# Gate products of a gated MLP as filler beside attention, with their gelu built from tanh

## The chip, the cores and the metric

The kernel runs on one core of a Trainium2 chip. The metric is the device time of one launch in microseconds, as the median of three runs. TensorE (PE) multiplies, VectorE (DVE), ScalarE (ACT) and GpSimd (POOL) work on its results, and SyncE (SP) issues the DMAs. Each engine works through its own queue of instructions in order and waits on semaphores where an instruction needs another engine's result.

## The reference

Two transformer blocks of two layers each, width 1024, float32. The first block mixes three attention branches and a convolutional feed-forward. The second, where most of the change lies, has 256 latent and 256 context tokens; in its last layer the context gives keys and values alone. The gated branch `chunk_gmlp` and the attention share one output product:

```python
def chunk_gmlp(u, vg, w_s, b_s, g_norm):
    u = gelu(u)
    vg = group_layernorm(gelu(vg).reshape(b, n, 4, 128), g_norm)     # 4 groups of 128
    mixed = einsum('gpq,bnqgc->bnpgc', w_s, chunks of 128 rows of vg) + b_s
    return u * mixed.reshape(b, n, 512)

for l in range(2):
    z = modulate(rmsnorm(x), ...) @ w_in[l]          # q | k | v | u | vg
    attn = softmax(q k^T) v                          # 8 query heads of 64, 2 kv heads, after rmsnorm and rope
    x = x + gate1 * (concat([attn, chunk_gmlp(u, vg, ...)]) @ w_out[l])
    x = x + gate2 * (relu(modulate(rmsnorm(x), ...) @ w_ff1[l])**2 @ w_ff2[l])
```

## The kernel before

**Products.** Every float32 product is three TensorE products of operands split into a rounded part hi and a remainder lo (`mm3`: L157 hi by hi, L158 and L159 with one lo). Weights come as raw tiles of 128x2048 into three buffers (`load_w`); ScalarE casts pieces of 1024 columns to hi (L147) and VectorE subtracts to get lo (L149). Activations are split the same way by `split` (L181 on ScalarE, L182 on VectorE). Products of a layer's weights go to PSUM tiles called acc, scores to s, transposed probabilities to pt, attention output to o.

**Order.** The program is written as Python generators, and a scheduler puts each engine's instructions in order, the earlier traced with the higher priority, as operands come free. `weave(main, side, ratio)` draws steps of a filler `side` after each step of `main`, `ratio` of them on average, and what is left at the end.

**A layer of block 2.** After q, k and v come the products of vg, in two halves of two groups (`g_half`, 4 row tiles of 128 in layer 0, 2 in layer 1; a Gelu on ScalarE for each, L970). Then VectorE takes mean and variance of every group (bn_stats L1049, bn_aggr L1050), a reciprocal root is formed on POOL, and the groups are normalised (L1055). `u_tasks` makes the four gate tiles of u: for each, 8 contraction steps of 3 products for each stream (latents, and in layer 0 context too), so 192 products of 256 columns in layer 0 and 96 in layer 1, and one Gelu on ScalarE (L1066). All four are traced ahead of attention. Then `weave(attn(), fill, WV2[l])` runs attention, 16 steps in layer 0 and 8 in layer 1, with a filler: four mix tiles (`mix_tasks`, 32 or 16 small products L1077, then the gate's factor L1083 and a split) and the half of w_out's products that reads the gated branch (`out_half(1)`, eight tiles). The other half, `out_half(0)`, follows attention.

**An attention step.** For a pair of heads and a block of queries: scores s (six products), their maximum (L1099 or L1103, VectorE), its scaling (L1107), exp on ScalarE with its sum (L363), the sum's reciprocal (L371), the scaling of the probabilities on ScalarE (L374), and `pair_out`: four transposes into pt (L388), a split of pt (L181, L182) and six products with v into o, as many rounds as there are pairs of key blocks. `pair_out` serves block 1 too.

Other lines: L257 are modulation products on VectorE, which are traced as side work (`prep`, `mod_rate`), L1044 the final norm's factors of block 1's output.

Of the kernel before, what the change touches and what calls it, by code (L numbers as in the profile page):

```python
# [19 lines left out]
P = 128  # L20
# [16 lines left out]

PIN = (False, True, True, False)

WV2 = (0.78, 1.62)  # L40

NMR = 2

# [4 lines left out]
WL = (1.0, 0.75)  # L48

PIPE = 1  # L50

WV = (0.34, 1.48, 0.48)

# [18 lines left out]
def program(tc, A, out, stop=None):  # L72
# [4 lines left out]
    def mk(pool, shape, dtype=F32, tag=None, bufs=None):  # L77
        count[0] += 1
        kw = {} if bufs is None else {"bufs": bufs}
        return pool.tile(shape, dtype, tag=tag, name=f"{tag}_{count[0]}", **kw)  # L80

    top = ExitStack()
    with top:
# [205 lines left out]
        def cut(s):  # L289
            return slice(s * T, (s + 1) * T)  # L290
# [27 lines left out]
        def run(gen):  # L318
            for _ in gen:
                pass  # L320
# [58 lines left out]
        def pair_out(po, ps, v, n):  # L379

            for g in range(0, n, 2):
                pt = mk(pst, [P, 512], tag="pt")
                for k in range(2):
                    for i in range(2):
                        o = (2 * k + i) * P
                        PE.transpose(pt[:, o : o + P], ps[i][:, (g + k) * P : (g + k + 1) * P], ident)  # L388
                hi, lo = mk(top_pt[0], [P, 512], F32R, **top_pt[1]), mk(top_pt[0], [P, 512], F32R, **top_pt[2])
                split(pt, hi, lo)  # L390
                for k in range(2):
                    c = slice(k * T, k * T + T)
                    mm3(po, v(g + k), (hi[:, c], lo[:, c]), g + k == 0, g + k == n - 1)

        def pair_split(po, hi, lo):

# [429 lines left out]
        def block2():  # L826
            with ExitStack() as st:
# [32 lines left out]
                def mm_x(ps, piece, x, n):  # L860
                    mm_w(ps[:, 0:n], piece, 0, KD, lambda k: x(k, slice(0, n)))
# [9 lines left out]
                for l in range(L):  # L871
# [89 lines left out]
                    def g_half(c, w):  # L961
                        if not vg:
                            vg.append(u8([P, 4, 512]))
                        for b in range(NB):
                            ps = acc()[:, :T]
                            x, bs = (hl, hc)[b // 2], slice(b % 2 * P, b % 2 * P + P)
                            for k in range(KD):
                                mm3(ps, x(k, bs),
                                    at(w[k // 4], slice(None), slice(k % 4 * T, k % 4 * T + T)), k == 0, k == KD - 1)
                            S.activation(vg[0][:, b, c * T : (c + 1) * T], ps, AF.Gelu_apprx_tanh)  # L970
                            yield

                    if l == 0:
                        hc, e, al, wk = glob["start"]
# [62 lines left out]
                    for _ in g_half(0, wg):  # L1037
                        next(prep, None)
                    wu = load_w(A["w_in2"][l, 3], 1024, 2048)
                    weave(g_half(1, wg2), prep, 1.0)  # L1040
                    vg = vg[0]
                    if l == 0:
                        for k in range(KD):
                            V.scalar_tensor_tensor(xx[:, k, LAT], xx[:, k, LAT], glob["fing"][:, k : k + 1], frow[:, 0, :], op0=ALU.mult, op1=ALU.mult)  # L1044
                    mv = mk(kp, [P, 4, 4, 2], tag="mv", bufs=1)
                    for b in range(NB):
                        for g in range(4):
                            bn = small([P, 6], tag="bn", bufs=2)
                            V.bn_stats(bn, vg[:, b, g * P : (g + 1) * P])  # L1049
                            V.bn_aggr(mv[:, b, g, :], bn)  # L1050
                    rv = rsqrt(mv[:, 0:NB, :, 1], [P, NB, 4], 1.0, EPS)
                    for b in range(NB):
                        for g in range(4):
                            gs = slice(g * P, (g + 1) * P)
                            V.tensor_scalar(vg[:, b, gs], vg[:, b, gs], mv[:, b, g, 0:1], rv[:, b, g : g + 1],  # L1055
                                            op0=ALU.subtract, op1=ALU.mult)
                    u = u8([P, 4, 512])

                    def u_tasks():
                        for c in range(2):  # L1060
                            w = load_w(A["w_in2"][l, 4], 1024, 2048) if c else wu
                            for mi in range(2):
                                ps = acc()
                                for s in streams:
                                    mm_x(ps[:, cut(s)], w[mi], (hl, hc)[s], T)
                                S.activation(u[:, 2 * c + mi, full], ps[:, full], AF.Gelu_apprx_tanh)  # L1066
                                yield


                    gm = []  # L1070

                    def mix_tasks():
                        gm[:] = [u8p()]
                        for g in range(4):
                            ps = acc()[:, :N]
                            for b in range(NB):
                                PE.matmul(ps[:, b * P : (b + 1) * P], vg[:, b, g * P : (g + 1) * P], wsT[:, g, :], start=True, stop=True)  # L1077
# [5 lines left out]
                            V.tensor_mul(t[:, :N], t[:, :N], u[:, g, full])  # L1083
                            split(t[:, :N], *gm[0](g, full))
                            yield


                    def attn():
# [59 lines left out]
                    def gate(m, ps, cols):  # L1148
                        update(m, ps, 2, cols)

                    fill = chain(mix_tasks(), out_half(1, lambda k, c: gm[0](k, c), gate))
                    run(u_tasks())
                    mod_rate(R2[1])
                    ya = u8p()
                    weave(attn(), fill, WV2[l])

                    def products(ap, x, cols_list, use, first=None):
# [215 lines left out]
```

## Time and profile before

| | |
|---|---|
| median of 3 runs | 1806.24 us (1802.46, 1806.24, 1807.23) |
| the profiled execution | 1804.39 us, span 1802.6 us |
| mean granted TensorE clock | 0.993 |
| PE, DVE, ACT busy | 97%, 80%, 56% of the span |
| layer 0's attention in block 2 | 1000.0 to 1098.6 us |
| layer 1's attention in block 2 | 1533.4 to 1607.3 us |

The two stretches run from the first scores to the first products with finished attention output. PE busy is the union of the matmuls' modelled durations; matmuls overlap, so their number in a window says more than their busy time. DVE and ACT busy times are sums over instructions that don't overlap.

### The profile page before, as it was taken

The numbers are of one execution on the slowest core, as the hardware profiler recorded it, in microseconds if no ns is written. First come the engines' busy times: TensorE is split into PE (matmuls) and PEld (weight loads), VectorE is DVE, ScalarE is ACT, GpSimd is POOL, SyncE is SP. The second block draws the span as 40 slices with busy tenths as digits, with TensorE's granted clock in tenths as the row PEclk, the third lists the DMA queues.
The fourth block names the chain that finished last, engine by engine and source line by source line (L and its number), as shares of the span: only waits on it lengthen the run. The fifth ranks groups of instructions, "written<-read, shape, count | busy, mean of one in ns | idle before, by whom it ended". The sixth has DMA issues, their size and how long they took to land.

```text
span 1802.6 us, 33988 instructions
## 1 busy us (share of the span) xinstructions
PE 1750.1 (97%) x13352; PEld 1669.1 (93%) x13352; DVE 1449.8 (80%) x3142; ACT 1014.0 (56%) x1994; POOL 83.0 (5%) x85
## 2 busy tenths in 40 slices
PE   7999999999999999999999899999999999799999
PEld 6999999999999999999999677989898989689999
DVE  7996989889898788988778676988676768777665
ACT  5866656665585665766554575515151536665553
POOL 0100210000010021000012000000000001000000
PEclk9999999999999999999999999999999999999999
DMA  7364664557545456554533221554545443225552
GB/s 283 123 212 165 211 233 171 186 164 257 197 159 199 163 183 246 185 190 158 195 138 119 71 71 36 168 201 154 185 149 191 141 151 117 71 72 209 187 187 94
DMA packets 68096, 297.10 MB, mean 165 GB/s; under 512 B 7648, under 2 KB 11104, under 8 KB 42336
## 3 DMA queue, kind: packets, MB, share of 16 engines
q1 hardware_dynamic: 67936, 294.93, 47.4%
q8 instruction: 105, 1.72, 0.4%
q14 instruction: 55, 0.45, 0.1%
HBM read 293.85 MB, written 1.05 MB: 164 GB/s over the span
## 4 chain that ended last, share of the span: by engine, by line
PE 82%; DVE 9%; ACT 5%; issue 2%; POOL 1%; DMA 1%; SPq 0%; POOLq 0%; ACTq 0%; DVEq 0%
PE acc L157 24%; PE acc L158 23%; PE acc L159 23%; DVE lo L149 2%; PE s L157 2%; PE s L158 2%; PE s L159 2%; PE pt L388 1%; ACT hi L147 1%; DVE u L182 1%; PE o L158 1%; ACT p L363 1%; DVE mjunk L257 1%; ACT p L374 1%; PE o L157 1%
## 5 line engine op out<-in xcount | busy, mean ns | idle before, releaser
L157 PE MATMUL acc<-u,hi 128*128 128x256 f32 (+2 forms) x3604 | 1052.3, 293 | 17.5 <-ACT hi L147 10.3
L159 PE MATMUL acc<-u,lo 128*128 128x256 f32 (+2 forms) x3604 | 1048.7, 292 | 2.6 <-DVE lo L149 2.4
L158 PE MATMUL acc<-u,hi 128*128 128x256 f32 (+2 forms) x3604 | 1051.0, 292 | 0.0
L147 ACT CAST hi<-raw 128x1024 fp32r<-128x1024 f32 (+2 forms) x470 | 473.6, 1010 | 452.9 <-PE acc L158 383.8
L157 PEld LDWEIGHTS acc<-u,hi 128*128 128x128 f32 x3604 | 682.6, 190 | 33.5 <-ACT hi L147 11.4
L159 PEld LDWEIGHTS acc<-u,lo 128*128 128x128 f32 x3604 | 682.4, 190 | 16.7 <-DVE lo L149 4.2
L158 PEld LDWEIGHTS acc<-u,hi 128*128 128x128 f32 x3604 | 683.6, 190 | 13.6 <-DVE u L182 0.6
L149 DVE TENSOR_TENSOR lo<-raw,hi 128x1024 fp32r<-128x1024 f32 (+2 forms) x470 | 552.0, 1182 | 104.5 <-ACT hi L147 100.7
L257 DVE CUSTOM_DVE_ANT_0 mjunk<-mraw,csil,c_par 128x512 bf16<-128x512 f32 x160 | 120.7, 754 | 10.5 <-DMA mraw<-in_w_mod 9.8
L257 DVE CUSTOM_DVE_ANT_0 mjunk<-mraw,csil,mpart 128x512 bf16<-128x512 f32 x160 | 120.8, 755 | 7.9 <-DMA mraw<-in_w_mod 6.5
L1130 DVE SCALAR_TENSOR_TENSOR xx<-acc,mods,xx 128x256 f32<-128x256 f32 x144 | 64.7, 479 | 55.4 <-PE acc L159 55.2
L868 ACT ACTIVATE nt<-nt,shb 128x256 f32<-128x256 f32 x96 | 48.7, 510 | 61.0 <-DVE nt L867 60.9
L181 ACT CAST u<-nt 128x256 fp32r<-128x256 f32 x146 | 57.3, 405 | 41.0 <-DVE nt L1212 33.3
L195 POOL TENSOR_TENSOR rs_y<-rs_v,mhalf 128x2 f32<-128x2 f32 (+2 forms) x26 | 30.9, 1188 | 1019.3 <-DVE rs_v L193 1019.3
L182 DVE TENSOR_TENSOR u<-nt,u 128x256 fp32r<-128x256 f32 x146 | 59.4, 421 | 17.0 <-ACT u L181 15.6
L159 PE MATMUL s<-u,lo 128*128 128x256 f32 x224 | 62.9, 281 | 0.5 <-DVE lo L149 0.5
L157 PE MATMUL s<-u,hi 128*128 128x256 f32 x224 | 62.7, 280 | 0.0
L158 PE MATMUL s<-u,hi 128*128 128x256 f32 x224 | 62.7, 280 | 0.0
L1212 DVE TENSOR_TENSOR nt<-nt 128x256 f32<-128x256 f32 x96 | 40.5, 423 | 19.1 <-ACT nt L868 13.1
L157 PE MATMUL acc<-hi,u 128*128 128x256 f32 (+1 forms) x168 | 48.6, 289 | 0.0
L182 DVE TENSOR_TENSOR kf<-pt,kf 128x512 fp32r<-128x512 f32 x40 | 27.5, 688 | 26.2 <-ACT kf L181 26.0
L159 PE MATMUL acc<-hi,u 128*128 128x256 f32 (+1 forms) x168 | 48.2, 287 | 0.0
(243 smaller groups left out, 2048.7 us busy)
## 6 DMA issues: line engine op xcount, KB each, us to landing
raw<-in_w_ff SPq DMA_DIRECT2D x64, 1024.0 KB, 4.9
raw<-in_w_in SPq DMA_DIRECT2D x61, 1024.0 KB, 4.9
mraw<-in_w_mod SPq DMA_DIRECT2D x192, 256.0 KB, 3.4
raw<-in_w_up SPq DMA_DIRECT2D x44, 1024.0 KB, 4.9
raw<-in_w_down SPq DMA_DIRECT2D x32, 704.0 KB, 4.2
raw<-in_w_out SPq DMA_DIRECT2D x16, 1024.0 KB, 4.9
raw<-in_w_br SPq DMA_DIRECT2D x12, 1024.0 KB, 4.9
nbias<-in_na_bias SPq DMA_DIRECT2D x8, 384.0 KB, 3.0
```

The costliest lines, as they stand in the source:

```text
L147: S.copy(hi[:, : b - a], raw[:, a:b])
L149: last_lo[0] = V.tensor_sub(lo[:, : b - a], raw[:, a:b], hi[:, : b - a].bitcast(F32))
L157: PE.matmul(ps, a[0], b[0], start=start, stop=False)
L158: PE.matmul(ps, a[0], b[1], start=False, stop=False)
L159: return PE.matmul(ps, a[1], b[0], start=False, stop=stop)
L181: S.copy(hi, src)
L182: return V.tensor_sub(lo, src, hi.bitcast(F32))
L195: G.tensor_tensor(y, v, mhalf[:, :n] if len(shape)==2 else mhalf[:, :n].rearrange('p (a b) -> p a b', b=shape[2]), op=ALU.pow)
L257: V.tensor_tensor_reduce(out=junk, in0=w, in1=csil[:, i, half * 512 : half * 512 + 512], op0=ALU.mult, op1=ALU.add, scale=1.0, scalar=part ...
L868: S.activation(dst, dst, func, bias=b)
L1130: V.scalar_tensor_tensor(xx[:, m, cut(s)], ps[:, s * T - cols.start : s * T - cols.start + T], md[i][:, m, s : s + 1], xx[:, m, cut(s)], o ...
L1212: V.tensor_mul(r, r, r)
```

## The change

The four gate tiles leave the place ahead of attention and become steps of the filler, one step for each stream of a tile, each tile followed by the mix of the group before it. PRE takes one such step (layer 0) or two (layer 1) before attention starts, and WV2 changes. The gate's gelu is no longer one ScalarE instruction but its tanh form in five: Square and Tanh on ScalarE (L1074, L1077), and on VectorE a tensor_scalar (L1075), a multiply (L1076) and a scalar_tensor_tensor (L1078), the last two of which read the product from PSUM; the factor 0.5 goes into the mix (L1105). Statistics of vg are taken behind each product and the root for each half; the first half is normalised within the second half's products, the second half behind the first gate tile. The value products in `pair_out` get a priority lower by 40 (PVO), in block 1 too. The attention output goes into the buffers of q, and the buffer for all of u goes.

```diff
-WV2 = (0.78, 1.62)
+WV2 = (1.0, 1.55)
+PRE = (1, 2)
+PVO = 40
+GC = float(np.sqrt(2.0 / np.pi))
...
                 split(pt, hi, lo)
-                for k in range(2):
-                    c = slice(k * T, k * T + T)
-                    mm3(po, v(g + k), (hi[:, c], lo[:, c]), g + k == 0, g + k == n - 1)
+                with tc.high_priority(offset=-PVO):
+                    for k in range(2):
+                        c = slice(k * T, k * T + T)
+                        mm3(po, v(g + k), (hi[:, c], lo[:, c]), g + k == 0, g + k == n - 1)
...
                             S.activation(vg[0][:, b, c * T : (c + 1) * T], ps, AF.Gelu_apprx_tanh)
+                            for g in range(2):
+                                bn = small([P, 6], tag="bn", bufs=2)
+                                V.bn_stats(bn, vg[0][:, b, c * T + g * P : c * T + (g + 1) * P])
+                                V.bn_aggr(mv[:, b, g, :], bn)
                             yield
+                        rv = rsqrt(mv[:, 0:NB, :, 1], [P, NB, 2], 1.0, EPS)
+                        norms.append((mv, rv))
...
-                    weave(g_half(1, wg2), prep, 1.0)
-                    vg = vg[0]
+                    second = g_half(1, wg2)
+                    for _ in range(2):
+                        next(second)
+                        next(prep, None)
+                    normalise(0)
+                    weave(second, prep, 1.0)
...
-                    u = u8([P, 4, 512])
-
-                    def u_tasks():
-                        for c in range(2):
-                            w = load_w(A["w_in2"][l, 4], 1024, 2048) if c else wu
-                            for mi in range(2):
-                                ps = acc()
-                                for s in streams:
-                                    mm_x(ps[:, cut(s)], w[mi], (hl, hc)[s], T)
-                                S.activation(u[:, 2 * c + mi, full], ps[:, full], AF.Gelu_apprx_tanh)
-                                yield
...
+                    def twice_gelu(dst, x, n):
+
+                        th = tmp()[:, :n]
+                        S.activation(th, x, AF.Square)
+                        V.tensor_scalar(th, th, 0.044715 * GC, GC, op0=ALU.mult, op1=ALU.add)
+                        V.tensor_mul(th, th, x)
+                        S.activation(th, th, AF.Tanh)
+                        V.scalar_tensor_tensor(dst, th, 1.0, x, op0=ALU.add, op1=ALU.mult)
...
+                        def gate_tile(g):
+                            nonlocal w
+                            if g == 2:
+                                w = load_w(A["w_in2"][l, 4], 1024, 2048)
+                            us[g], ps = tmp(), acc()
+                            for s in streams:
+                                mm_x(ps[:, cut(s)], w[g % 2], (hl, hc)[s], T)
+                                if s != streams[-1]:
+                                    yield
+                            twice_gelu(us[g][:, full], ps[:, full], N)
+                            yield
...
+                            V.scalar_tensor_tensor(t[:, :N], t[:, :N], 0.5, us.pop(g)[:, full], op0=ALU.mult, op1=ALU.mult)
+                            split(t[:, :N], *gm(g, full))
+
+                        for g in range(4):
+                            yield from gate_tile(g)
+                            if g == 0:
+                                normalise(1)
+                            if g:
+                                mix(g - 1)
+                        mix(3)
...
-                    fill = chain(mix_tasks(), out_half(1, lambda k, c: gm[0](k, c), gate))
-                    run(u_tasks())
+                    fill = chain(mix_tasks(), out_half(1, gm, gate))
                     mod_rate(R2[1])
-                    ya = u8p()
+                    ya = q
+                    for _ in range(PRE[l]):
+                        next(fill)
                     weave(attn(), fill, WV2[l])
```

Lines move by three before `pair_out`'s priority and by more behind it: L157 becomes L160, L182 L185, L388 L391, L1077 (mix) L1099, L1099 (maximum) L1128, L1055 L991.

**TensorE where layer 0's attention begins.** Before, the last gate tile (acc_13271) is complete, two score tiles follow, then all of the mix, and the second step's scores:

```order
L159 MATMUL acc_13271<-u_2022_11446,lo_13211 128x256
L157 MATMUL s_13324<-kk_12190,u_2173_12407 128x512
L158 MATMUL s_13324<-kk_12190,u_2173_12407 128x512
L159 MATMUL s_13324<-kk_12190,u_2174_12408 128x512
L157 MATMUL s_13329<-kk_12190,u_2173_12407 128x512
L158 MATMUL s_13329<-kk_12190,u_2173_12407 128x512
L159 MATMUL s_13329<-kk_12190,u_2174_12408 128x512
L1077 MATMUL acc_13450<-wsT_12188,u_2239_12721 128x128 x4
L1077 MATMUL acc_13492<-wsT_12188,u_2239_12721 128x128 x4
L1077 MATMUL acc_13543<-wsT_12188,u_2239_12721 128x128 x4
L1077 MATMUL acc_13656<-wsT_12188,u_2239_12721 128x128 x4
L157 MATMUL s_13346<-kk_12190,u_2173_12407 128x512
```

With the change this is the place of the second step's scores (s_13151 and s_13156; the first step's stand 36 rows earlier, amid gate tile 0). Gate tile 1 (acc_13292) lies around them:

```order
L160 MATMUL acc_13292<-u_2200_12576,hi_12934 128x256
L161 MATMUL acc_13292<-u_2200_12576,hi_12934 128x256
L162 MATMUL acc_13292<-u_2200_12576,lo_12935 128x256
L160 MATMUL s_13151<-kk_12190,u_2173_12407 128x512
L161 MATMUL s_13151<-kk_12190,u_2173_12407 128x512
L162 MATMUL s_13151<-kk_12190,u_2174_12408 128x512
L160 MATMUL acc_13292<-u_2200_12576,hi_12934 128x256
L160 MATMUL s_13156<-kk_12190,u_2173_12407 128x512
L161 MATMUL s_13156<-kk_12190,u_2173_12407 128x512
L162 MATMUL s_13156<-kk_12190,u_2174_12408 128x512
L161 MATMUL acc_13292<-u_2200_12576,hi_12934 128x256
```

Gate products that stood ahead of all scores now stand between and behind them; mix comes later.

**VectorE where the first maximum of layer 0 is taken.** Before:

```order
L257 ISA mods_16_106 128x1
L1099 TENSOR_REDUCE nm_13323<-s_13324 128x1
L149 TENSOR_TENSOR lo_14247<-raw_14244,hi_14246 128x1024
L1099 TENSOR_REDUCE nm_13323<-s_13329 128x1
L1107 TENSOR_TENSOR nm_2318_13334<-nm_13323,sc_12194 128x2
L371 RECIPROCAL rsum_13341<-sum_13338 128x2
L1099 TENSOR_REDUCE nm_13345<-s_13346 128x1
```

With the change (L196 starts the second half's reciprocal root, L991 normalises its groups, L260 is modulation):

```order
L152 TENSOR_TENSOR lo_13768<-raw_13765,hi_13767 128x1024
L196 TENSOR_SCALAR rs_v_13082<-mv_12945 128x8
L1128 TENSOR_REDUCE nm_13128<-s_13129 128x1
L1128 TENSOR_REDUCE nm_13128<-s_13134 128x1
L991 TENSOR_SCALAR u_2239_12721<-u_2239_12721,mv_12945,rs_y_13084 128x128
L1136 TENSOR_TENSOR nm_2309_13139<-nm_13128,sc_12194 128x2
L991 TENSOR_SCALAR u_2239_12721<-u_2239_12721,mv_12945,rs_y_13084 128x128 x7
L260 ISA mjunk_13445,mpart_13440<-mraw_13441,csil_100,c_par_31_139 128x512
```

A lo piece and the second half's root now stand before the first maximum, and its normalisations around the scaling L1136 and behind it.

**ScalarE and VectorE at gate tile 0 of layer 0** (kf_13227 holds the square and then the tanh, acc_13103 the products). ScalarE with the change:

```order
L184 CAST kf_13193<-pt_13188 128x512
L1074 ACTIVATE kf_13227<-acc_13103 128x512
L1077 ACTIVATE kf_13227<-kf_13227 128x512
L150 CAST hi_14026<-raw_14024 128x1024
L366 ACTIVATE kf_13241,sum_13242<-s_13234,nm_2332_13239,sc_12194 128x256 x2
L184 CAST kf_13254<-pt_13249 128x512
L377 ACTIVATE kf_13241<-kf_13241,rsum_13245 128x256 x2
L184 CAST kf_13269<-pt_13264 128x512
```

and VectorE:

```order
L185 TENSOR_TENSOR kf_13194<-pt_13188,kf_13193 128x512
L1075 TENSOR_SCALAR kf_13227<-kf_13227 128x512
L1136 TENSOR_TENSOR nm_2346_13323<-nm_13317,sc_12194 128x2
L260 ISA mjunk_13786,mpart_13781<-mraw_13782,csil_100,c_par_31_139 128x512
L260 ISA mpart_13781 128x1
L1076 TENSOR_TENSOR kf_13227<-kf_13227,acc_13103 128x512
L1078 SCALAR_TENSOR_TENSOR kf_13102<-kf_13227,acc_13103 128x512
L152 TENSOR_TENSOR lo_14027<-raw_14024,hi_14026 128x1024
```

Tanh stands right behind Square on ScalarE, and the two VectorE passes that it needs have a scaling and a modulation product (L260) between them; exps and casts of transposes stand behind Tanh. Before, a Gelu (L1066) ahead of attention stood for the five gelu rows.

**TensorE in the last steps of layer 1's attention.** Before, the transposes of the next round (pt_19889) follow the last value product of the round before:

```order
L158 MATMUL o_19815<-kf_19880,vv_18565 128x256
L159 MATMUL o_19815<-kf_19879,vv_18565 128x256
L157 MATMUL o_19815<-kf_19879,vv_18565 128x256
L158 MATMUL o_19815<-kf_19880,vv_18565 128x256
L159 MATMUL o_19815<-kf_19879,vv_18565 128x256
L388 MATMUL pt_19889<-ident_84,kf_19806 128x128
L388 MATMUL pt_19889<-ident_84,kf_19807 128x128
L388 MATMUL pt_19889<-ident_84,kf_19806 128x128
L388 MATMUL pt_19889<-ident_84,kf_19807 128x128
L157 MATMUL o_19815<-kf_19894,vv_18565 128x256
L158 MATMUL o_19815<-kf_19895,vv_18565 128x256
```

With the change they (pt_19941) come ahead of most value products of their predecessor (o_19896 from kf_19918):

```order
L160 MATMUL o_19896<-kf_19917,vv_18591 128x256
L161 MATMUL acc_20049<-u_3390_18731,hi_19990 128x256
L162 MATMUL acc_20049<-u_3390_18731,lo_19991 128x256
L160 MATMUL acc_20049<-u_3390_18731,hi_19990 128x256
L161 MATMUL acc_20049<-u_3390_18731,hi_19990 128x256
L162 MATMUL acc_20049<-u_3390_18731,lo_19991 128x256
L160 MATMUL acc_20049<-u_3390_18731,hi_19990 128x256
L391 MATMUL pt_19941<-ident_84,kf_19887 128x128
L391 MATMUL pt_19941<-ident_84,kf_19888 128x128
L391 MATMUL pt_19941<-ident_84,kf_19887 128x128
L391 MATMUL pt_19941<-ident_84,kf_19888 128x128
L161 MATMUL o_19896<-kf_19918,vv_18591 128x256
```

## Rows read from the trace of the kernel before

**Rows 1.** Page, part 1: busy time, share of the span, number of instructions.

```profile
PE 1750.1 (97%) x13352; PEld 1669.1 (93%) x13352; DVE 1449.8 (80%) x3142; ACT 1014.0 (56%) x1994; POOL 83.0 (5%) x85
```

**Rows 2.** Windows: PE, PEld, DVE, ACT, POOL busy (number); clock, DMA, GB/s.

```profile
970.00:980.00 10.00, 10.00 (x87) 10.00 (x86) 10.00 (x42) 3.15 (x5) 0.00 (x0) 1.00 0.47 159
1010.00:1020.00 10.00, 6.46 (x39) 4.69 (x38) 4.91 (x11) 5.57 (x15) 0.00 (x0) 1.00 0.01 2
1060.00:1070.00 10.00, 10.00 (x60) 8.48 (x59) 7.65 (x18) 6.36 (x13) 0.00 (x0) 1.00 0.12 29
1090.00:1100.00 10.00, 8.30 (x45) 6.25 (x44) 3.93 (x8) 5.03 (x13) 0.00 (x0) 0.97 0.01 2
```

**Rows 3.** Matmuls by line and shape, 977.5:1000: busy, mean ns, idle before.

```profile
L158 PE MATMUL acc<-u,hi 128*128 128x256 f32 x63 | 17.8, 282 | 0.0
```

**Rows 4.** Timeline, start of layer 0's attention: start, duration, instruction, idle before.

```profile
999.99 0.40 PE L157 MATMUL s<-kk,u 128*128 128x512 f32 x1
...
1000.23 0.39 PE L158 MATMUL s<-kk,u 128*128 128x512 f32 x1
...
1000.89 0.69 DVE L1099 TENSOR_REDUCE nm<-s 128x1 f32<-128x512 f32 x1 [0.58 <-PE s L159]
...
1006.36 0.27 PE L388 MATMUL pt<-ident,kf 128*128 128x128 f32 x1
```

**Rows 5.** Timeline of matmuls in the filled part of layer 0's attention.

```profile
1056.27 0.60 PE L388 MATMUL pt<-ident,kf 128*128 128x128 f32 x4
1056.63 0.48 PE L157 MATMUL acc<-u,hi 128*128 128x512 f32 x1
```

**Rows 6.** Matmuls by line and shape, layer 0's attention, 1000:1098.6.

```profile
L157 PE MATMUL acc<-u,hi 128*128 128x512 f32 x44 | 17.5, 416 | 1.2 <-ACT u L181 1.2
L388 PE MATMUL pt<-ident,kf 128*128 128x128 f32 x96 | 15.5, 280 | 0.7 <-ACT kf L374 0.6
L158 PE MATMUL o<-kf,vv 128*128 128x256 f32 x48 | 14.9, 310 | 4.2 <-DVE kf L182 4.2
...
L157 PE MATMUL s<-kk,u 128*128 128x512 f32 x24 | 10.8, 451 | 1.1 <-ACT kf L363 1.1
...
L1077 PE MATMUL acc<-wsT,u 128*128 128x128 f32 x32 | 3.7, 275 | 0.0
```

**Rows 7.** The same for its filled part, 1050:1090.

```profile
L158 PE MATMUL acc<-u,hi 128*128 128x512 f32 x29 | 11.7, 402 | 0.0
...
L388 PE MATMUL pt<-ident,kf 128*128 128x128 f32 x43 | 6.5, 272 | 0.0
...
L158 PE MATMUL o<-kf,vv 128*128 128x256 f32 x22 | 6.4, 290 | 0.0
...
L157 PE MATMUL s<-kk,u 128*128 128x512 f32 x10 | 4.5, 452 | 0.0
```

**Rows 8.** Window in layer 1's attention, columns as in rows 2.

```profile
1550.00:1560.00 10.00, 7.33 (x33) 5.50 (x33) 5.58 (x13) 6.63 (x15) 0.00 (x0) 0.83 0.35 135
```

**Rows 9.** Timeline of layer 1's attention: first scores, first transpose, casts at the end.

```profile
1533.48 0.39 PE L157 MATMUL s<-kk,u 128*128 128x512 f32 x1
...
1549.69 0.33 PE L388 MATMUL pt<-ident,kf 128*128 128x128 f32 x1 [0.39 <-ACT kf L374]
...
1600.46 0.59 ACT L181 CAST kf<-pt 128x512 fp32r<-128x512 f32 x1 [2.21 <-PE pt L388]
...
1603.16 0.59 ACT L181 CAST kf<-pt 128x512 fp32r<-128x512 f32 x1 [2.11 <-PE pt L388]
```

**Rows 10.** VectorE by line and shape, 1000:1098.6.

```profile
L182 DVE TENSOR_TENSOR kf<-pt,kf 128x512 fp32r<-128x512 f32 x24 | 16.5, 689 | 13.8 <-ACT kf L181 13.6
...
L149 DVE TENSOR_TENSOR lo<-raw,hi 128x1024 fp32r<-128x1024 f32 x5 | 6.1, 1214 | 0.0
```

**Rows 11.** VectorE by line and shape, layer 1's attention, 1533.4:1607.3.

```profile
L1055 DVE TENSOR_SCALAR u<-u,mv,rs_y 128x128 f32<-128x128 f32 x8 | 2.1, 340 | 1.8 <-POOL rs_y L195 1.8
```

**Rows 12.** ScalarE by line and shape, 1000:1098.6.

```profile
L1066 ACT ACTIVATE u<-acc 128x512 f32<-128x512 f32 x1 | 0.6, 591 | 0.0
```

More of the change, by code (lines that the diff above doesn't have):

```diff
@@ L963, in g_half @@
                             vg.append(u8([P, 4, 512]))
+                        mv = mk(kp, [P, 4, 2, 2], tag="mv", bufs=2)
                         for b in range(NB):
@@ L970, in g_half, with normalise @@
                             S.activation(vg[0][:, b, c * T : (c + 1) * T], ps, AF.Gelu_apprx_tanh)
+                            for g in range(2):
+                                bn = small([P, 6], tag="bn", bufs=2)
+                                V.bn_stats(bn, vg[0][:, b, c * T + g * P : c * T + (g + 1) * P])
+                                V.bn_aggr(mv[:, b, g, :], bn)
                             yield
+                        rv = rsqrt(mv[:, 0:NB, :, 1], [P, NB, 2], 1.0, EPS)
+                        norms.append((mv, rv))
+                    norms = []
+                    def normalise(c):
+                        mv, rv = norms[c]
+                        for b in range(NB):
+                            for g in range(2):
+                                t = vg[0][:, b, c * T + g * P : c * T + (g + 1) * P]
+                                V.tensor_scalar(t, t, mv[:, b, g, 0:1], rv[:, b, g : g + 1], op0=ALU.subtract, op1=ALU.mult)
                     if l == 0:
@@ L1044, in block2 @@
                             V.scalar_tensor_tensor(xx[:, k, LAT], xx[:, k, LAT], glob["fing"][:, k : k + 1], frow[:, 0, :], op0=ALU.mult, op1=ALU.mult)
[L1045 to L1056, printed above, removed]
-                    u = u8([P, 4, 512])
-                    def u_tasks():
-                        for c in range(2):
-                            w = load_w(A["w_in2"][l, 4], 1024, 2048) if c else wu
-                            for mi in range(2):
-                                ps = acc()
-                                for s in streams:
-                                    mm_x(ps[:, cut(s)], w[mi], (hl, hc)[s], T)
-                                S.activation(u[:, 2 * c + mi, full], ps[:, full], AF.Gelu_apprx_tanh)
-                                yield
@@ L1070, in block2 @@
-                    gm = []
-                    def mix_tasks():
-                        gm[:] = [u8p()]
-                        for g in range(4):
+                    gm = u8p()
+                    def twice_gelu(dst, x, n):
[5 more added lines that the diff above has]
+                        V.scalar_tensor_tensor(dst, th, 1.0, x, op0=ALU.add, op1=ALU.mult)
@@ new lines, in mix_tasks, with mix @@
+                    def mix_tasks():
+                        us, w = {}, wu
+                        def gate_tile(g):
[9 more added lines that the diff above has]
+                            yield
+                        def mix(g):
@@ L1075, in mix_tasks @@
                             ps = acc()[:, :N]
                             for b in range(NB):
-                                PE.matmul(ps[:, b * P : (b + 1) * P], vg[:, b, g * P : (g + 1) * P], wsT[:, g, :], start=True, stop=True)
+                                PE.matmul(ps[:, b * P : (b + 1) * P], vg[0][:, b, g * P : (g + 1) * P], wsT[:, g, :], start=True, stop=True)
                             t = tmp()
@@ L1082, in mix_tasks @@
                                                    op0=ALU.mult, op1=ALU.add)
-                            V.tensor_mul(t[:, :N], t[:, :N], u[:, g, full])
-                            split(t[:, :N], *gm[0](g, full))
-                            yield
+                            V.scalar_tensor_tensor(t[:, :N], t[:, :N], 0.5, us.pop(g)[:, full], op0=ALU.mult, op1=ALU.mult)
[7 more added lines that the diff above has]
+                        mix(3)
                     def attn():
```

## Prediction

> **What bounds the kernel now.** I read the page's engine totals first, then the attention stages of block 2 in ten-microsecond windows, then the matmuls of such a stage by shape, and last its timeline. TensorE is shown busy for 97% of the span [rows 1], but a matmul's row lasts longer than the step to the next, so a busy TensorE may still have holes. I therefore count. In layer 0's attention 1010:1020 holds 39 matmuls where 1060:1070 holds 60 of much the same mixture [rows 2].
>
> The steps between starts: 190 products of 256 columns fill 22.5 us, 0.118 us each [rows 3]; one of 512 columns takes 0.24 (999.99 to 1000.23) [rows 4], over many such pairs 0.231; four transposes 0.36, so 0.09 each [rows 5]. Layer 0's stage, 1000.0 to 1098.6, holds (44 acc + 24 s) x 3 x 0.231 = 47.1, 48 x 3 o x 0.118 = 17.0, 96 pt x 0.09 = 8.6 and 32 mix products, 3.7: 76.4 us of matmul work (one row stands for the three products of a split) [rows 6]. So 22.2 of 98.6 us are holes. From 1050 to 1090, where w_out's products fill in, it is 85 acc (29, 29 and 27) + 30 s at 0.231, 66 o at 0.118 and 43 pt at 0.09: 38.2 of 40 us, 95.5% [rows 7]. The holes therefore lie in the first 50 us, about 18, and in the last 8.6, about 2 (45 matmuls in 1090:1100 against 60) [rows 2]. Early attention has little filler: the four gate tiles ran before it, and mix and w_out's products are all that is left.
>
> The idle column of [rows 6] adds up to only 7.2 us, and taken at its word it caps what layer 0 can win there at 7. The Trainium skill (Perfetto Trace Analysis, Identifying the Most-Contended Engine) calls matmul busy share a poor measure of what is left, and weight-load busy a better one. The trace agrees: in 1010:1020 matmuls are busy 6.46 us, weight loads 4.69, and the count gives less than either [rows 2]. With the cap the sum below would be some 3 us smaller.
>
> Layer 1's stage, half as many steps, is thin too: 33 matmuls in 1550:1560 [rows 8]. Its first scores start at 1533.48 and its first transpose at 1549.69 [rows 9], 16.2 us, because gate tiles 2 and 3 stand between the two halves of the first scores; layer 0 needs 6.4 (999.99 to 1006.36) [rows 4].
>
> **The change, part by part.** TensorE's instructions stay the same in number.
>
> *Gate products as filler, layer 0.* 192 products x 0.118 = 22.7 us [rows 3] ran from 977.3 on. Now 24 (2.8 us) precede the first scores, which so begin at 980.1; 168 (19.8 us) join the stage, whose work is then 96.2. VectorE decides the start: it is full in 970:980 [rows 2], and statistics, eight normalisations (0.34 each [rows 11]), modulation and three lo pieces (1.21 each [rows 10]) stand ahead of the first reduce. I put that reduce 7 us after the scores (bounds: 0.9, as at 1000.89, and 11, the whole list). From reduce to first transpose it took 5.5 us [rows 4]: the transpose comes at 992.6, 12.5 us in. (The scaled maximum that exp waits for, L1136, now has one normalisation before it that waits for POOL's rsqrt; the two reduces, 1.4 us, cover most of that.) Ahead of it TensorE has 12 score and about 42 gate products, 7.7 us; 4.8 are a hole. Then 88.5 us of work remain, 6.6 of it in the last 8.6 us, which stay bare. The other 81.9 at 95.5% would take 85.8. But VectorE and ScalarE get busier. A gate tile needs a tensor_scalar, a multiply and a scalar_tensor_tensor, at most 0.69 each by the 512-column row that reads PSUM [rows 10], 8.3 us for four; with normalisations, lo pieces and seven or so modulation products VectorE has about 20 us more. ScalarE gets a Square and a Tanh a tile, at 0.59 like the Gelu [rows 12], 4.7 us. I take 93% (bounds 88 and 95.5%), nearest to the dense row: 88.1 us, so the stage ends at 980.1 + 12.5 + 88.1 + 8.6 = 1089.3, against 1098.6: **-9.3** (-4 at 88%; -15 with a prompt reduce and 95.5%).
>
> The Trainium skill (VectorE: DVE Perf Modes, Why PSUM operands drop a tier) lets an fp32 tensor_scalar on SBUF take two elements a cycle, and anything that reads PSUM one. By it one of the three passes costs half of the 0.69, 1.4 us less in four tiles; the sum would stay, as VectorE isn't taken to be the bound. No row here shows that form at 512 columns.
>
> *Layer 1.* The scores start where they did, both halves at once; tiles 2 and 3 follow. VectorE's list puts the first reduce, I estimate as in layer 0, some 5.5 us behind, the first transpose at 1544.5 (bounds 1540 and 1549). That alone is no gain, as TensorE has less to do meanwhile. Before, 12 scores, 44 gate and 16 mix products, 9.8 us in 16.2, left 6.4 of holes; now 12 scores, 4 mix and 19 gate products, 5.5 in 11.0, leave 5.5: -0.9. The 29 gate products behind it, 3.4 us, go into steps that had no filler [rows 8]: -3.4.
>
> *Value products at lower priority.* The next transposes now go out ahead of value products. In a bare round transpose, cast, lo and value products follow each other, 2.70 us from cast to cast (1600.46 to 1603.16) [rows 9]; with the transposes first, five or six products of 0.118, 0.6 us, leave the loop. Four such rounds at the end of layer 1: -2.4. In layer 0 it is within the 93%. Block 1 uses the same function, beside denser filler: -1 (from -4 to +3, as a value product may now be late for what reads it).
>
> *Edits at nothing.* Statistics per product, the dropped u buffer, q's buffers for the output (a pair's q is read before it is overwritten) and the 0.5 in the mix have VectorE's free 25 to 50% as cover [rows 2]; without it they would cost 2 us. PRE and WV2 set where the filler stands, which the counts include. The second rsqrt on POOL runs beside products.
>
> Sum: -9.3 - 0.9 - 3.4 - 2.4 - 1 = -17.0. The profiled execution took 1804.39 us, 1.85 below the median: 1787.4 on its own scale, 1789.2 on the median's. I say **1788**. The ends: layer 0 -4 to -15, layer 1 -2 to -11, block 1 +3 to -4, together -3 to -30.
>
> **Rivals.** *(A) All holes fill.* With a prompt reduce and 95.5% layer 0 gives -15, layer 1 -11, block 1 -4: 1805 - 30 = **1775**. For it: 1050 to 1090 is that dense. Against it: VectorE's list at the start. Chance 0.10.
>
> *(B) VectorE paces.* It is busy 0.77 of 1060:1070 [rows 2], and 20 us more over a stage of some 109 add 0.18: 0.95, and in each step reduce, a small product, a reciprocal and two lo passes lie in line. Against it: the filler needs VectorE seldom, and statistics only move. At 85% density layer 0 gives -1, layer 1 -3: **1801**. Chance 0.13.
>
> *(C) ScalarE parked, slower.* A tile's Tanh stands right behind its Square on ScalarE, but needs two VectorE passes in between, with other VectorE work among them; exps and the transposes' casts queue behind it, and TensorE waits for both. In tile 0 it is two passes of at most 0.69 and a modulation product that I put at 1: 2.4 us. My 93% holds some 0.6 of it per tile. The gain is used up where the eight tiles cost 17.0 / 8 + 0.6 = 2.7 us each on the chain; from 3.4 it is slower by over 0.3%. With a lo piece of 1.21 in front of each, 3.6: 1788 + 8 x 3.0 = **1812**. For it: VectorE's lo passes of the transposes already wait 13.6 us for ScalarE [rows 10]. Against it: matmuls for some us usually stand ready. Chance 0.07.
>
> *(D) Nothing moves*, the scheduler keeping gate products ahead: **1806**. The order shows gate 1 among scores. Chance 0.02.
>
> **How the numbers follow.** Forecast 0.68, with its own range of 1780 to 1799; A 0.10, B 0.13, C 0.07, D 0.02. A measurement of this kernel tells about 0.3%, 5.4 us, from no change, so faster means below 1800.8. Faster: forecast, A and a third of B, 0.82; same: the rest of B and D, 0.10; slower: C and a tail of block 1, 0.08. The range 1775 to 1802 takes in A's and B's times and leaves out C, D and some tails.
>
> **What would show it.** In the changed profile layer 0's first scores should start near 980 and its first transpose near 993; the windows behind it should hold 55 to 70 matmuls (gate products are the short ones) where they held 36 to 57; its first w_out products with attention output should come near 1089. Layer 1 should take some 6 to 7 us less from first scores to last value product. Wrong, if Tanh has over 2 us of idle time before it and casts wait behind it (C), if VectorE is full from 990 to 1080 (B), or if the first reduce is over 11 us late. A later end of block 1, before 900, would put the fault with the value products' priority.

## The result, and the profile after

The changed kernel takes 1790.6 us (median of four, 1786.2 to 1791.2) against 1804.95: 0.9919 of the kernel before, 95% interval 0.9904 to 0.9934. A second set of runs on another chip gave 0.9933 (0.9920 to 0.9947). The forecast was 1788, in a range of 1775 to 1802.

Page of the changed kernel, part 1 (answers to [rows 1]), whose busy share has hardly moved:

```profile
PE 1745.6 (98%) x13352; PEld 1670.0 (93%) x13352; DVE 1457.3 (81%) x3168; ACT 1017.9 (57%) x2002; POOL 82.5 (5%) x87
```

Ten-microsecond windows of its layer 0 attention, 980.3 to 1090.6 (columns as in [rows 2]; PEclk is the third number from the end):

```profile
980.00:990.00 10.00, 6.01 (x41) 5.45 (x40) 9.38 (x29) 1.74 (x5) 1.64 (x1) 0.96 0.41 131
990.00:1000.00 10.00, 10.00 (x64) 8.97 (x62) 9.31 (x26) 6.92 (x14) 0.00 (x0) 0.87 0.45 157
1000.00:1010.00 10.00, 10.00 (x80) 9.48 (x79) 6.21 (x12) 7.63 (x19) 0.00 (x0) 1.00 0.10 29
...
1030.00:1040.00 10.00, 7.14 (x42) 5.36 (x42) 8.00 (x16) 7.38 (x19) 0.00 (x0) 1.00 0.08 28
1040.00:1050.00 10.00, 10.00 (x41) 7.80 (x42) 6.87 (x13) 4.68 (x10) 0.00 (x0) 0.83 0.10 27
```

The early windows now hold up to 80 matmuls, short gate products among them. Two thin places are left, at the start and around 1040. What TensorE waited for in that stretch (total us, times, longest), and then in layer 1's:

```profile
PE s L160 <- ACT kf L366: 4.3, 2, 4.0
PE acc L160 <- DVE kf L1078: 1.8, 1, 1.8
```

```profile
PE acc L160 <- DVE kf L1078: 2.1, 1, 2.1
PE acc L1099 <- DVE kf L1078: 2.0, 2, 1.5
PE o L161 <- DVE kf L185: 1.7, 3, 1.0
```

The first is the start: scores need a score tile back from exp, and exp waits for a maximum that VectorE takes late. L1078 is the last pass of a gate's tanh chain, which alone gives the tile's accumulator back. The timeline of the start (answers to [rows 4]):

```profile
980.26 0.39 PE L160 MATMUL s<-kk,u 128*128 128x512 f32 x1
...
986.13 1.28 DVE L1128 TENSOR_REDUCE nm<-s 128x1 f32<-128x512 f32 x2
...
988.49 0.78 ACT L366 ACTIVATE kf<-s,nm,sc 128x512 f32<-128x512 f32 x1 [8.26 <-DVE nm L1136]
...
989.41 0.79 PE L160 MATMUL s<-kk,u 128*128 128x512 f32 x1 [3.99 <-ACT kf L366]
```

Scores at 980.26, maximum 5.9 us later, first transpose at 993.31; layer 0's stage ends at 1090.61 with the first w_out product that needs the last pair's attention output (as 1098.62 does before), 8.0 us earlier than before. Layer 1's stage takes 70.2 us (1523.06 to 1593.25) where it took 73.8. The stretch between the two is 2.4 us shorter, the one behind them 0.7 longer. Up to here the forecast looks confirmed.

### The profile page after: what moved, and what is told of

Read it like the earlier page. It is cut to its first block, busy times and chain, and to the rows that moved or that the text cites. A ratio compares the mean times of both kernels' runs of the same rounds, so it can differ in the third digit from the quotient of the medians.

```text
span 1789.3 us, 34042 instructions
## 1 busy us (share of the span) xinstructions
PE 1745.6 (98%) x13352; PEld 1670.0 (93%) x13352; DVE 1457.3 (81%) x3168; ACT 1017.9 (57%) x2002; POOL 82.5 (5%) x87
## 4 chain that ended last, share of the span: by engine, by line
PE 80%; DVE 11%; ACT 5%; issue 1%; POOL 1%; DMA 1%; SPq 0%; POOLq 0%; ACTq 0%; DVEq 0%
PE acc L160 23%; PE acc L162 23%; PE acc L161 23%; DVE lo L152 3%; PE s L160 2%; PE s L161 2%; PE s L162 2%; PE pt L391 1%; ACT hi L150 1%; DVE u L185 1%; POOL rs_y L198 1%; DMA raw<-in_w_in 1%; ACT p L366 1%; ACT p L377 1%; PE o L160 1%
## 5 line engine op out<-in xcount | busy, mean ns | idle before, releaser
L160 PE MATMUL acc<-u,hi 128*128 128x256 f32 (+2 forms) x3604 | 1054.1, 293 | 17.0 <-ACT hi L150 10.3
L150 ACT CAST hi<-raw 128x1024 fp32r<-128x1024 f32 (+2 forms) x470 | 473.6, 1010 | 440.8 <-PE acc L161 377.9
L160 PEld LDWEIGHTS acc<-u,hi 128*128 128x128 f32 x3604 | 683.5, 190 | 33.4 <-ACT hi L150 11.4
L260 DVE CUSTOM_DVE_ANT_0 mjunk<-mraw,csil,mpart 128x512 bf16<-128x512 f32 x160 | 119.9, 749 | 13.0 <-DMA mraw<-in_w_mod 11.9
L260 DVE CUSTOM_DVE_ANT_0 mjunk<-mraw,csil,c_par 128x512 bf16<-128x512 f32 x160 | 119.8, 749 | 7.5 <-DMA mraw<-in_w_mod 6.5
L198 POOL TENSOR_TENSOR rs_y<-rs_v,mhalf 128x2 f32<-128x2 f32 (+2 forms) x29 | 35.1, 1213 | 1028.3 <-DVE rs_v L196 1028.3
L185 DVE TENSOR_TENSOR u<-nt,u 128x256 fp32r<-128x256 f32 x146 | 59.5, 422 | 17.9 <-ACT u L184 16.5
L160 PE MATMUL s<-u,hi 128*128 128x256 f32 x224 | 62.7, 280 | 0.0
L160 PE MATMUL acc<-hi,u 128*128 128x256 f32 (+1 forms) x168 | 48.5, 289 | 0.0
L161 PE MATMUL acc<-lo,u 128*128 128x256 f32 (+1 forms) x168 | 48.1, 286 | 0.0
```

The source lines that it names most:

```text
L150: S.copy(hi[:, : b - a], raw[:, a:b])
L185: return V.tensor_sub(lo, src, hi.bitcast(F32))
L198: G.tensor_tensor(y, v, mhalf[:, :n] if len(shape)==2 else mhalf[:, :n].rearrange('p (a b) -> p a b', b=shape[2]), op=ALU.pow)
L260: V.tensor_tensor_reduce(out=junk, in0=w, in1=csil[:, i, half * 512 : half * 512 + 512], op0=ALU.mult, op1=ALU.add, scale=1.0, scalar=part ...
```

## The experiments

Every ratio is to the kernel before on the same chip, with its 95% interval.

**1. Gate products ahead of attention again**, all else as changed:

```diff
-WV2 = (1.0, 1.55)
+WV2 = (0.5, 1.0)
-PRE = (1, 2)
+PRE = (8, 4)
```

> The changed kernel with all gate steps taken ahead of attention (PRE of 8 and 4, and what is left of the filler spread evenly: WV2 of 0.5 and 1.0); tanh gelu, statistics per product, value products' priority and q's buffers stay. If the gain comes from gate products that fill holes: layer 0's first scores are back near 1000, its stage ends near 1098, and most of the 14 us are gone, 1798 to 1804. If it comes from the other parts (value products' priority, spread statistics, buffers): within 3 us of the changed kernel's 1790.6, so below 1794.

Measured 0.9958 (0.9946 to 0.9971), 1794.6 us. About half of the gain goes, between the two expectations. First scores came at 1007.42, later than before, because half of the mix products (16 of 32) and the tanh chains went ahead with the gate tiles, and a gate tile there waited for the chain's last pass:

```profile
1000.21 0.55 PE L160 MATMUL acc<-u,hi 128*128 128x256 f32 x1 [3.89 <-DVE kf L1078]
```

So this run mixes two things.

**2. The value products at their own priority**, all else as changed:

```diff
-PVO = 40
+PVO = 0
```

> The changed kernel with the value products at their own priority again (PVO 0). By my sum the lower priority is worth 2.4 us in layer 1's bare rounds (2.7 us a round again), something in layer 0 and 1 in block 1: 1792 to 1796. If it carries the gain: 1799 or more. If it does nothing: 1789 to 1792.

Measured 0.9991 (0.9980 to 1.0001): without it nothing of the gain can be told from no change. Its stages: layer 0 ends at 1094.49, layer 1 takes 74.9 us, 1.2 longer than before.

**3. That priority alone**, on the kernel before:

```diff
+PVO = 40
...
                 split(pt, hi, lo)
-                for k in range(2):
-                    ...
+                with tc.high_priority(offset=-PVO):
+                    for k in range(2):
+                        ...
```

> The kernel before with nothing but the value products' lower priority. By my sum 3 us less than before, 1800 to 1803, most of it in the last steps of layer 1's attention. If this carries the gain: 1796 or less. If the lower priority hurts block 1: 1806 or more, with a later end of block 1.

Measured 0.9916 (0.9903 to 0.9930): the whole gain, from one line, with gate tiles, statistics, gelu and buffers as before. My theory of the gain falls here. The kernel before has in the early steps of layer 0 (ScalarE's casts of transposes; start, duration, idle before):

```profile
1012.09 0.59 ACT L181 CAST kf<-pt 128x512 fp32r<-128x512 f32 x1 [1.28 <-PE pt L388]
...
1014.82 0.56 ACT L181 CAST kf<-pt 128x512 fp32r<-128x512 f32 x1
...
1018.14 0.59 ACT L181 CAST kf<-pt 128x512 fp32r<-128x512 f32 x1 [2.76 <-PE pt L388]
...
1020.85 0.59 ACT L181 CAST kf<-pt 128x512 fp32r<-128x512 f32 x1
```

and with the priority alone:

```profile
1009.09 0.59 ACT L182 CAST kf<-pt 128x512 fp32r<-128x512 f32 x1 [0.69 <-PE pt L389]
...
1011.15 0.59 ACT L182 CAST kf<-pt 128x512 fp32r<-128x512 f32 x1 [0.37 <-PE pt L389]
...
1013.21 0.59 ACT L182 CAST kf<-pt 128x512 fp32r<-128x512 f32 x1 [0.67 <-PE pt L389]
...
1015.27 0.59 ACT L182 CAST kf<-pt 128x512 fp32r<-128x512 f32 x1 [0.37 <-PE pt L389]
```

A round takes 2.06 us in place of 2.7 to 3.3. The pass that takes lo (VectorE) and what TensorE does around it show why. The kernel before, and the priority alone:

```profile
1012.70 0.69 DVE L182 TENSOR_TENSOR kf<-pt,kf 128x512 fp32r<-128x512 f32 x1 [1.14 <-ACT kf L181]
...
1012.72 0.38 PE L157 MATMUL o<-kf,vv 128*128 128x256 f32 x1 [0.68 <-ACT kf L181]
1013.45 0.38 PE L158 MATMUL o<-kf,vv 128*128 128x256 f32 x1 [0.34 <-DVE kf L182]
...
1014.14 0.60 PE L388 MATMUL pt<-ident,kf 128*128 128x128 f32 x4
```

```profile
1009.71 0.69 DVE L183 TENSOR_TENSOR kf<-pt,kf 128x512 fp32r<-128x512 f32 x1 [0.57 <-ACT kf L182]
...
1010.46 0.66 PE L389 MATMUL pt<-ident,kf 128*128 128x128 f32 x4 [0.34 <-DVE kf L183]
1010.87 0.36 PE L159 MATMUL o<-kf,vv 128*128 128x256 f32 x1
1011.07 0.28 PE L160 MATMUL o<-kf,vv 128*128 128x256 f32 x1
```

There is one PSUM tile pt, and lo is the last pass that reads it. So the end of lo releases two things at once: the value product that needs lo, and the next round's transposes, which write pt. Before, the value product stood first and four more behind it, and the transposes began 0.69 us after it (1013.45, 1014.14). With the priority the transposes begin 0.06 us behind the end of lo (1010.40, 1010.46), and the value products run while ScalarE casts the next tile. The transposes had not been ready while TensorE waited for lo (in run 3 their row names lo's pass as what they waited for); what left the loop is the five value products between lo and the transposes.

Layer 0's stage takes 90.7 us (997.58 to 1088.29) in place of 98.6, layer 1's 69.0 in place of 73.8. In layer 0 the four gaps between casts at the start of each of the first three pairs of heads shrank from 38.3 to 28.7 us together; the other eleven gaps grew by 1.6.

**4. One Gelu in place of the tanh chain**, in the filler (the mix's factor 0.5 becomes 1.0):

```diff
-                        th = tmp()[:, :n]
-                        S.activation(th, x, AF.Square)
-                        ...
+                        S.activation(dst, x, AF.Gelu_apprx_tanh)
```

> The changed kernel with one Gelu on ScalarE for each gate tile in place of the five tanh steps, at the same place in the filler. The program now has 19 table loads where it had 7. If ScalarE's chain matters: 12 loads of 1.28 us, 15 us more on ScalarE amid exps, less about 4 us of Squares, and Tanh's waits of 1.3 to 1.9 us each go: 4 to 10 us slower than the changed kernel, 1794 to 1801. If VectorE paces the stages, three passes a tile less (1.8 us of VectorE in layer 0, about 1.1 in layer 1) win more than the loads cost: 1789 or less.

Measured 0.9932 (0.9918 to 0.9945), like the changed kernel's 0.9919 and 0.9933; both expectations missed. Each of the six tiles amid attention costs ScalarE two loads, one piece of 3.2 us (layer 1's first two stand ahead of its first exp and need none of their own):

```profile
996.77 1.28 ACT L1073 ACT_TABLE_LOAD   x1
998.07 0.60 ACT L1073 ACTIVATE kf<-acc 128x512 f32<-128x512 f32 x1
998.67 1.28 ACT L366 ACT_TABLE_LOAD   x1
```

The tanh form costs ScalarE about as much, since Tanh waits for VectorE (changed kernel, gate tiles 0 and 2 of layer 0):

```profile
1001.30 0.63 ACT L1077 ACTIVATE kf<-kf 128x512 f32<-128x512 f32 x1 [1.93 <-DVE kf L1076]
...
1026.43 0.63 ACT L1077 ACTIVATE kf<-kf 128x512 f32<-128x512 f32 x1 [1.28 <-DVE kf L1076]
```

0.60 + 1.28 to 1.93 + 0.63 is 2.5 to 3.2 us. The tanh form thus buys no measurable time here.

**5. The start repaired**: lo pieces and the second half's normalisations wait for the first scaled maximum, in the changed kernel (`load_w` holds lo pieces back until `pin`):

```diff
-                            if g == 0:
-                                normalise(1)
+                            if g == 2:
+                                with tc.issue_after(pin[0].ins):
+                                    normalise(1)
...
-                            if last and (j, side, b) == (0, 0, 0):
+                            if (j, side, b) == (0, 0, 0):
                                 pin[0] = ins
```

> The changed kernel with VectorE's list ahead of layer 0's first maximum shortened: three lo pieces and the second half's normalisations are held back until the first step's scaled maximum. If the hole of 4.0 us ahead of the second step's scores costs time of the stage: first transpose near 989 to 990 in place of 993.3, 2 to 4 us less than the changed kernel (ratio to the kernel before 0.990 or below where the changed kernel has 0.9919). If the filler that fills the hole is only missing later: no change within 1.5 us.

Measured 0.9908 (0.9893 to 0.9922). The first transpose came 8.2 us after the first scores (981.65 to 989.84), where it took 13.05, and the wait for exp fell to 0.3 us. Against the changed kernel's two measurements that is 1 to 2.5 thousandths; by the intervals alone it could be none.

**6. The accumulator freed early**, in the changed kernel:

```diff
                         th = tmp()[:, :n]
+                        S.copy(dst, x)
+                        x = dst
                         S.activation(th, x, AF.Square)
```

> The changed kernel with each gate tile copied from PSUM to SBUF by ScalarE first, so that the accumulator is free after one instruction; the tanh chain reads the copy. The changed kernel's trace has 1.8 us (layer 0) and 4.1 us (layer 1) of TensorE waits for the chain's last pass (L1078). If these waits are why layer 1 gained only 3.6 us: 2 to 5 us less than the changed kernel, 0.987 to 0.991 of the kernel before. If ScalarE, which gets 8 copies (3.9 us), sets the pace: 0 to 3 us more.

Measured 0.9901 (0.9887 to 0.9915). Waits for the chain's last pass are gone from both stages; layer 0's ends at 1084.11, layer 1's takes 69.3 us. The interval overlaps that of the changed kernel's first measurement, and lies clear of the second. In layer 1 a wait came up in their place, for lo of gate tiles 2 and 3, which the last layer holds back until its first scaled maximum:

```profile
PE acc L162 <- DVE lo L152: 4.9, 1, 4.9
```

**7. Both repairs.**

> The two edits before together. If holes at the start and accumulator waits are what the gate move still loses: 1782 to 1786 on the changed kernel's scale, below the kernel before with the value products' priority alone (0.9916). If not: 0.991 to 0.993, as the changed kernel.

Measured 0.9863 (0.9849 to 0.9876), 1777.3 us, clear of every run above. Layer 0's stage ends at 1078.94.

**8. The value products' priority in block 2 alone**, on the kernel before (shown against run 3; `in2` is set where block 2 begins):

```diff
+                in2[0] = True
...
-                with tc.high_priority(offset=-PVO):
+                with tc.high_priority(offset=-PVO) if in2[0] else nullcontext():
```

> The kernel before with the value products' lower priority in block 2 only. If the gain is the bare transpose-cast-lo-value rounds of block 2's attention, where a round took 2.7 us and takes 2.06: 13 to 16 us less than before, as with the priority everywhere (0.9916). If block 1 has a share: 0.993 to 0.995.

Measured 0.9920 (0.9906 to 0.9934): block 1 has no share that can be told. Layer 0's first scores came at 997.21 here too, 2.8 us before those of the kernel before, though TensorE, VectorE and ScalarE have the same instructions in the same order ahead of them, so single profiles vary by that much.

**9. Both repairs without the priority** (PVO = 0).

> The kernel with both repairs (early first maximum, gate copy) but the value products at their own priority (PVO 0). The change without that priority was 0.9991, with it 0.9919. If gate products only fill holes once the repairs let them, and this is separate from the priority: 0.9925 to 0.9950, a gain of 9 to 13 us without any change of order in the rounds. If the repairs help only where the rounds are short: 0.996 to 0.999.

Measured 0.9929 (0.9917 to 0.9942). The change without the priority, worth nothing in run 2, is worth some 12 us once start and accumulators are repaired. The last casts of layer 1 still stand 2.7 to 3.2 us apart:

```profile
1580.89 0.59 ACT L184 CAST kf<-pt 128x512 fp32r<-128x512 f32 x1 [1.84 <-PE pt L391]
...
1583.59 0.59 ACT L184 CAST kf<-pt 128x512 fp32r<-128x512 f32 x1 [2.12 <-PE pt L391]
...
1586.75 0.59 ACT L184 CAST kf<-pt 128x512 fp32r<-128x512 f32 x1 [2.58 <-PE pt L391]
```

**10. Both repairs, and the weights of gate tiles 2 and 3 a tile earlier**:

```diff
+                            if g == 1:
+                                w2 = load_w(A["w_in2"][l, 4], 1024, 2048)
                             if g == 2:
-                                w = load_w(A["w_in2"][l, 4], 1024, 2048)
+                                w = w2
```

> The kernel with both repairs, and the weights of gate tiles 2 and 3 requested one tile earlier, in layer 1 so ahead of attention: their lo pieces are then not held back until the first maximum, for which TensorE waited 4.0 us there. If that wait is on the path: 3 to 5 us less than with both repairs alone, 0.983 to 0.985. If the first maximum comes later by as much as the lo pieces take (2.4 us): 0.985 to 0.9875.

Measured 0.9849 (0.9835 to 0.9862), 1774.9 us, the fastest of all, though its interval overlaps that of run 7. The wait of 4.0 us for lo falls to 1.0, but the first transpose of layer 1 comes 12.7 us after the scores where it came 10.5: some of it is given back at the first maximum, as the second expectation had it.

**11. The priority lowered by 8 in place of 40**, on the kernel before.

> The kernel before with the value products' priority lowered by 8 in place of 40. In the order the next transposes now pass the value products within a step only in part, and across steps hardly at all. If transposes ahead of value products are the gain: between no gain and 0.9916, about 0.994 to 0.998. If any lower priority does it by some other way (in block 1, or by moving filler): 0.991 to 0.993.

Measured 0.9958 (0.9946 to 0.9971): half. Casts in layer 0 stand 2.5 to 2.8 us apart (1007.48, 1009.97, 1012.71), between the two.

**12. The changed kernel on the chip of runs 9 to 11.**

> The changed kernel again, beside its repaired versions on one chip: 0.9904 to 0.9934 of the kernel before, as measured first. If the difference to the version with both repairs (0.9863) comes from chips and not from the kernel, it would lie below 0.989.

Measured 0.9933 (0.9920 to 0.9947), as said: runs 7 and 10 are faster than the change by more than the intervals.

## Why the prediction was right in its number and wrong in its reason

**Start of layer 0: right.** Scores 980.1 forecast, 980.26 seen; maximum 987.1, 986.13; transpose 992.6, 993.31; hole 4.8, wait 4.0 us; end 1089.3, 1090.61. Not right: the windows behind were to hold 55 to 70 matmuls, and 1030:1050 held 42 and 41.

**"Gate products as filler, layer 0, -9.3" fails as a cause.** Without the priority the whole rest of the change is worth 0.0009 +- 0.001 (run 2), with the priority nothing on top of it (0.9916 in run 3, 0.9919 and 0.9933 with the change). The step that failed is the one that took the 22.2 us of holes for missing filler. A part was the order of a round: value products stood between lo and the next transposes. TensorE's waits ahead of value products stood in the profile, 4.2 us for lo [rows 6] and 2.5 us for the cast, in a row that [rows 6] leaves out:

```profile
L157 PE MATMUL o<-kf,vv 128*128 128x256 f32 x48 | 14.8, 308 | 2.5 <-ACT kf L181 2.5
```

I used these rows for their idle sum alone, and with this one the sum is 9.7 us, not 7.2: the cap that the prediction took from it would not have cut the -9.3.

**"Value products at lower priority, -2.4 and -1" is the term that was mis-sized**: -15 us alone (run 3). The mechanism was right, 2.70 us to about 2.1 (2.21 and 2.06 in the changed kernel's end of layer 1). I counted four rounds and left those of layer 0 within the 93%; most of layer 0's 24 have it too, which the gaps between casts in run 3 show, and layer 1's stage as a whole lost 4.8 us.

**The number is luck.** The three terms for gate products, -13.6 together, brought nothing that can be told, and the priority brought 10 to 15 us (runs 2 and 3) in place of 3.4. The two errors nearly cancel.

**The two nearly add.** As first made, the rest of the change is worth nothing without the priority or with it. Repaired, it is worth 0.0071 without (run 9) and 0.0053 with it (run 7 against run 3): 0.9929 x 0.9916 is 0.9846, and run 7 measured 0.9863.

**Run 1** divides as follows. Its layer 0 stage takes 89.2 us (1007.42 to 1096.60), no longer than run 3's 90.7, which has the gate tiles ahead too. So filler missing in the stage is not what it lost; its first scores came 9.8 us later than run 3's, behind mix products and the wait for the tanh chain.

**Layer 1, -6.7 forecast, -3.6 seen.** The priority alone gave 4.8 there (run 3). The first transpose came 13.1 us after the scores, not 11.0, and 4.1 us of waits for the tanh chain's last pass had no term in the sum. I named what queues behind Tanh on ScalarE (C), not the accumulator that the chain holds; run 7 against run 5 shows that this cost time (0.9863, 0.9908), and run 9 with run 2 that both repairs together are worth 0.006.

**Block 1, -1:** nothing to be told (run 8). **Rival C:** Tanh waited 6.3 us in four tiles, 1.6 each in place of 2.4, and one in layer 1 waited 2.1, ahead of its first exp, without a loss against a native Gelu (run 4). **Rival B:** VectorE was busy 0.62 to 0.94 of the windows shown, and run 7 went faster with the same passes on it, so beyond the start, where its order made the first maximum late (run 5), it was not the bound. The Trainium skill (VectorE: DVE Perf Modes, Why PSUM operands drop a tier) caps an fp32 pass that reads PSUM at one element a cycle. In the changed kernel's trace the tensor_scalar, on SBUF, took 0.42 us, against 0.69 for the two passes that read PSUM:

```profile
L1078 DVE SCALAR_TENSOR_TENSOR kf<-kf,acc 128x512 f32<-128x512 f32 x4 | 2.8, 688 | 2.6 <-ACT kf L1077 2.6
...
L1075 DVE TENSOR_SCALAR kf<-kf 128x512 f32<-128x512 f32 x4 | 1.7, 420 | 0.0
```

That PSUM is what makes these two slower isn't shown, as in run 6 they read the SBUF copy and took as long:

```profile
L1078 DVE TENSOR_TENSOR kf<-kf,kf 128x512 f32<-128x512 f32 x4 | 2.8, 691 | 0.1
...
L1080 DVE SCALAR_TENSOR_TENSOR kf<-kf,kf 128x512 f32<-128x512 f32 x4 | 2.7, 685 | 0.0
```

**Run 2** is no faster than before though its layer 0 ends 4.1 us earlier: layer 1 gives 1.2 back, and the profile of the kernel before, at 1804.39, lies 2.3 above the median beside run 2. **Open:** how much of each gain came by the granted clock (last section).

## What to carry to other kernels

Before filling holes of an in-order engine, look at what one event releases there: where two instructions become ready together, the one that the other engines' chain waits for should stand first. Such a change of order can be worth more than filler, here 15 us for one line, against nothing for the filler as first made and 12 once repaired. When work moves beside a chain, ask what it holds while it waits, accumulators above all, and what it puts ahead of the chain's first instruction on each engine. A sum that comes out right proves none of its terms: run each part alone, on the kernel before too.

## What the hardware showed

The granted clock fell where TensorE had stood still, though not each time. In the changed kernel it is 0.87 in 990:1000, behind the wait of 4.0 us, and score products there start 0.43 us apart, near twice the 0.23 of full speed, as at 1.2 in place of 2.4 GHz:

```profile
980.26 0.39 PE L160 MATMUL s<-kk,u 128*128 128x512 f32 x1
...
980.49 0.40 PE L161 MATMUL s<-kk,u 128*128 128x512 f32 x1
...
990.00 0.63 PE L161 MATMUL s<-kk,u 128*128 128x512 f32 x1
...
990.43 0.63 PE L162 MATMUL s<-kk,u 128*128 128x512 f32 x1
```

So that hole cost more than its length. In the kernel before, 1010:1020 kept a clock of 1.00 with TensorE busy for 6.46 us [rows 2], and in 910:920, where run 8 has the same instructions in the same order, the clock differs (the kernel before, then run 8):

```profile
910.00:920.00 10.00, 9.09 (x71) 8.91 (x70) 5.79 (x14) 2.71 (x7) 2.94 (x3) 0.92 0.29 99
```

```profile
910.00:920.00 10.00, 9.09 (x77) 8.91 (x76) 6.61 (x15) 1.88 (x5) 2.94 (x3) 1.00 0.16 55
```

The clock is a part of the gains. Its mean over whole executions was 0.9947 in the kernel before and 0.9972 in run 3, and 0.9943 and 0.9995 beside and in run 10. If TensorE's clock set the pace throughout, these differences of 0.0025 and 0.0052 of some 1800 us are 4.5 of run 3's 15.9 us and 9.4 of run 10's 27.4: an estimate, and not separated by any run.

A table load took 1.28 us and the next instruction began 0.02 us behind it (run 4). The 12 loads that run 4 adds, 15 us of ScalarE's time, cost the kernel nothing that can be told.
